# Turning the gated head outputs to channels by transposing DMAs instead of TensorE

## The chip, the core and the metric

One core of a Trainium2 chip runs the whole layer. The metric is the device time of one execution in microseconds. PE is TensorE, DVE is VectorE, ACT is ScalarE, POOL is GpSimd, SP is SyncE, which mainly issues transfers.

## The reference

One decoder layer on 512 tokens of 1,024 channels: a norm, a wide input projection, a convolution branch, a gated linear attention branch (GLA), a gated merge, and a feed-forward block. The change touches the end of the GLA branch:

```python
o = _gla_chunked(qh, kh, vh, gkh)                 # 512 tokens x 4 heads x 256
o = o * lax.rsqrt(jnp.mean(o * o, axis=-1, keepdims=True) + EPS) * gla_norm_g[l]
o = o.reshape(bsz, seq, GLA_VDIM) * jax.nn.silu(r)
y_gla = o @ w_gla_out[l]
merged = jax.nn.sigmoid(gate_a) * y_conv + jax.nn.sigmoid(gate_b) * y_gla
```

## The kernel before

All matrix products are in fp32 with both operands split into a high part (rounded to fp32r) and a low part (the rest), so that a product is three matmuls (`mm3`, L537: the weight's low part with the activation's high part, high with low, high with high). Weights are loaded by SP as 512 KB tiles (`raw`, four buffers), ACT casts them into `whi`, DVE subtracts to get `wlo` (`split_weight`, L414). `order` (L244) is the list of weights in the order of use, and SP's queue takes the loads in this order as buffers come free (`load`, `refill`).

The head outputs `ot[t, n]` are held with tokens on partitions: t is one of four tiles of 128 tokens, n one of two halves of 512 channels. The gate r is computed by `seven("w_r", ...)` (L1453), a product with seven instead of eight half sized steps (`a11, a12, s1, n2, s4, n3, a22`). `put_r` (L1544) takes each finished piece: ACT applies silu, and DVE multiplies the piece before it into `ot` (L1561, the last one at L1565). The pieces finish in the order (t,n) = (0,0), (1,0), (0,1), (1,1), (2,1), (3,1), (2,0), (3,0).

The output projection (`tile_of("w_gla", m, ...)`, L1444) needs the result with channels on partitions. `gated_o(m, bank)` (L1246) does this for channel tile m: four 128x128 transposes on PE into a PSUM bank, then ACT multiplies by the norm's gain into the high part `hi` and DVE forms the low part `lo`. Eight such tiles are needed, m = 0 to 3 from n = 0 and m = 4 to 7 from n = 1. Two are turned at the end of the r stage (`r_at`), the others two at a time inside the following pair of merge gate tiles.

That pair is `pair_7(0)` (L1579): the gate tiles w_gb 6 and 7 computed together by `two_tiles` (L1344) in four parts called x1, x3, x2, x4. They are accumulated in the three PSUM banks x, y, z, in steps of twelve matmuls with 256 columns. Bank x is read out between its steps (`put` and `combine`, L1350 to L1354) while later steps keep adding to it, so a step on x waits for the readout of the step before. Behind the pair come the projection tiles w_gla 0 and 1 (`PLAIN_GLA`, L1628), then the pair w_ga 0 and 1. POOL forms sums of weight tiles for such pairs (L398). Within the engines a scheduler sets the order when the kernel is built; on the chip each engine runs its instructions in that order.

Of the kernel before, what the change touches and what calls it, by code (L numbers as in the profile page):

```python
# [11 lines left out]
F32R = mybir.dt.float32r  # L12
BF16 = mybir.dt.bfloat16
U8 = mybir.dt.uint8
AF = mybir.ActivationFunctionType
ALU = mybir.AluOpType

P = 128
# [82 lines left out]
def trunk_layer(ctx: ExitStack, tc: tile.TileContext, a: dict, out: bass.AP):  # L101
    nc = tc.nc

    def pool(name, bufs, space=None):
        kw = {"space": space} if space is not None else {}
        return ctx.enter_context(tc.tile_pool(name=name, bufs=bufs, **kw))
# [20 lines left out]
    def nm(s):  # L127
        return f"{s}_{next(names)}"
# [137 lines left out]
    for gi, pairs in enumerate(GROUPS):  # L266
# [6 lines left out]
        tight |= set(range(first, len(order)))  # L273
        order += [("w_down", (pairs, step, d)) for step, d in STEPS]
    ready, raws = [], []
    pair_raws = {}
    kept = {}
    used = [0]
# [2 lines left out]
    def load():  # L281
        if len(raws) < len(order):
            name, j = order[len(raws)]
            if name in SEVEN:
                raws.append(load_block(name, *j))
                return
            if name == "two":
                name, p, q, part = j
                if part == "x1":
                    pair_raws[name, p] = [raw_tile() for _ in range(2)]  # L290
                    for raw, m in zip(pair_raws[name, p], (p, q)):
                        nc.sync.dma_start(raw, a[name][m])
                raws.append(None)
                return
            raw = raw_tile()
            nc.sync.dma_start(raw, a[name][j])
            raws.append(raw)

    def refill():

# [241 lines left out]
        nc.tensor.matmul(acc, lh, rl, start=False, stop=False, **kw)  # L542
        nc.tensor.matmul(acc, lh, rh, start=False, stop=last, **kw)  # L543

    def col_tile(w, acts, acc=None, lo=0, hi=T, at={}, ks=range(KT)):

        if acc is None:
            acc = mm_bank()
        for k in ks:
            s = slice(k * P, (k + 1) * P)  # L550
            ah, al = acts[k]
            mm3(acc[:, lo:hi], (w[0][:, s], w[1][:, s]), (ah[:, lo:hi], al[:, lo:hi]), k == 0, k == KT - 1)
            if k in at:
                at[k]()
        return acc
# [687 lines left out]

    ot = {}

    def gated_o(m, bank):  # L1246
        po = bank()
        c = (m % 4) * P
        for p in range(NT):
            nc.tensor.transpose(po[:, p * P : (p + 1) * P], ot[p, m // 4][:, c : c + P], ident)  # L1250
# [5 lines left out]
        hi, lo = (both[:, 0, :], both[:, 1, :]) if m < 4 else (heap(F32R), heap(F32R))  # L1256
        nc.scalar.activation(hi, po, AF.Copy, scale=gain)
        low_at[:] = [nc.vector.scalar_tensor_tensor(lo, po, gain, hi.bitcast(F32), ALU.mult, ALU.subtract)]
        oa[m] = hi, lo

    part = [None] * KT

# [178 lines left out]
    merged_tiles = {}  # L1441
    outs = {"w_gla": (lambda: oa, gla_out), "w_conv": (lambda: ca, conv_out)}

    def tile_of(name, m, ks, acc=None):  # L1444
        if acc is None:
            acc = (weight(name, m), mm_bank())
        col_tile(acc[0], outs[name][0](), acc[1], ks=ks)
        if KT - 1 in ks:
            outs[name][1](m, acc[1])
        return acc  # L1450

# [88 lines left out]
    def sums_for(step):  # L1540
        while urgent and step in ("s1", "n2", "s4", "n3") and step not in merge_acts:
            urgent.pop(0)[1]()

    def put_r(step, t, n, acc):  # L1544
        if step in ("a11", "s1", "n2"):
            rt[t, n] = rp_.tile([P, T], F32, tag="r", name=nm("r"), bufs=6)
            return nc.scalar.copy(rt[t, n], acc)
        if step == "a22":
            rt[t, n] = rp_.tile([P, T], F32, tag="r", name=nm("r"), bufs=6)
            nc.scalar.activation(rt[t, n], acc, AF.Silu)  # L1550
        else:
            r = rt[t, n]
            one, two = (r, acc) if step == "n3" else (acc, r)
            done = nc.vector.tensor_tensor(r, one, two, ALU.add if step == "a12" else ALU.subtract)
            nc.scalar.activation(r, r, AF.Silu)
        if step == "a22":
            done = None
        with tc.issue_after(done.ins) if done else ExitStack():
            while gated:
                i, j = gated.pop()  # L1560
                nc.vector.tensor_tensor(ot[i, j], ot[i, j], rt[i, j], ALU.mult)  # L1561
        gated.append((t, n))
        if (step, t, n) == ("a22", 3, 0):
            i, j = gated.pop()
            nc.vector.tensor_tensor(ot[i, j], ot[i, j], rt[i, j], ALU.mult)  # L1565
        return done if step == "n3" else None

    def r_at(step, i):
        if (step, i) == ("a22", 1):
            for m in range(4, 6):  # L1570
                gated_o(m, ax_bank)

    seven("w_r", R_PAIRS, [ByTile(k) for k in range(4)], None, r_at, put=put_r, before=sums_for)
    half_of = [range(KT // 2), range(KT // 2, KT)]
    open_tiles = {}

# [2 lines left out]
    def pair_7(n):  # L1579
        (name, p, q), behind = MERGE[n], BEHIND[n]  # L1580
        unit = two_tiles(name, p, q, lambda: merge_acts, mm_bank, len(behind) < 3)
        if behind and behind[0][0] == "w_conv":
            while chains:
                fill(1)
        for j in range(4):
            while urgent and j and len(urgent) > (5 if j == 1 else 0):
                urgent.pop(0)[1]()
            done = next(unit)
            if n == 0 and j == 2:
                while len(after) > 1:  # L1590
                    fill(1)
            if n == 0 and j < 3:
                for m in ((6, 7), (0, 1), (2, 3))[j]:
                    gated_o(m, ax_bank)
                if j == 2:
# [426 lines left out]
```

## Time and profile before

| | us |
|---|---|
| time, median of 3 runs (lowest to highest) | 817.37 (816.91 to 817.74) |
| the profiled execution | 816.96 |
| its span, from the first to the last instruction | 815.3 |
| PE busy in the span | 807.5 |
| transposes of the gated outputs, first and last start | 284.2 and 296.2 |
| first projection tile w_gla begins | 297.70 |

Times in the timeline count from the span's start. Each row names the start, the length, the engine, the line, the operation, and output<-input. A matmul's length overlaps with the next one, so the step from start to start is what counts on PE. `SPq`, `ACTq` and `POOLq` are the issuing of transfers by these engines.

### The profile page before, as it was taken

To read this page: it belongs to the slowest core of one execution; us is meant where nothing else is said; L and a number is where in the kernel's file an instruction comes from. 1 tells how busy PE (TensorE), PEld (TensorE's weight loads), DVE (VectorE), ACT (ScalarE), POOL (GpSimd) and SP (SyncE) were. 2 spreads that over 40 slices of the span, in tenths; PEclk is the share of its full clock that TensorE was granted. 3 is DMA by queue.
4 is the path that set the end of the run, shared out by engine and by line. 5 is a ranking of instruction groups with operands and counts; after the bars stand their busy time and mean duration, and the time that the engine had idled before them with its cause. 6 is when DMAs were issued, how large, how long until landed. Compare 5 with 4: busy or idle time off the path is not lost.

```text
span 815.3 us, 11441 instructions
## 1 busy us (share of the span) xinstructions
PE 807.5 (99%) x4215; PEld 693.2 (85%) x4215; DVE 700.7 (86%) x1108; ACT 487.9 (60%) x746; POOL 192.5 (24%) x166
## 2 busy tenths in 40 slices
PE   9999999999999999999999999999999999999996
PEld 7888888788888898989888898898889988899885
DVE  6679999998998988486779899979976999789896
ACT  6667788677546575494435655556435663466655
POOL 2025433332204332122001100320133300522010
PEclk9999999999999999999999999999999999999999
DMA  8487858745831232432458613145732345334662
GB/s 337 146 198 179 187 160 176 161 119 135 186 95 60 78 130 78 137 105 95 164 124 220 190 57 126 52 154 156 144 127 92 142 117 167 105 104 171 165 129 105
DMA packets 36616, 113.60 MB, mean 139 GB/s; under 512 B 3704, under 2 KB 8960, under 8 KB 36560
## 3 DMA queue, kind: packets, MB, share of 16 engines
q1 hardware_dynamic: 29200, 86.92, 30.8%
q0 software_dynamic: 7200, 25.69, 18.0%
q8 instruction: 33, 0.54, 0.3%
q14 instruction: 23, 0.19, 0.1%
q10 hardware_dynamic: 160, 0.27, 0.1%
HBM read 110.76 MB, written 2.10 MB: 138 GB/s over the span
## 4 chain that ended last, share of the span: by engine, by line
PE 84%; DVE 13%; issue 1%; ACT 1%; DMA 1%; SPq 0%; DVEq 0%; ACTq 0%
PE mm L541 20%; PE mm L542 20%; PE mm L543 20%; DVE c L902 5%; PE cv L541 4%; PE cv L542 4%; PE cv L543 4%; DVE aside L902 3%; PE ax L542 2%; PE ax L541 2%; PE ax L543 2%; PE ax L1230 1%; PE ax L1232 1%; DMA kept<-in_w_r_dram 1%; PE ax L1212 0%
## 5 line engine op out<-in xcount | busy, mean ns | idle before, releaser
L541 PE MATMUL mm<-uh,wlo 128*128 128x512 f32 (+1 forms) x532 | 193.9, 364 | 0.2 <-DVE wlo L464 0.2
L542 PE MATMUL mm<-ul,whi 128*128 128x512 f32 (+1 forms) x532 | 191.6, 360 | 0.0
L543 PE MATMUL mm<-uh,whi 128*128 128x512 f32 (+1 forms) x532 | 191.4, 360 | 0.0
L427 DVE TENSOR_TENSOR wlo<-raw,whi 128x1024 fp32r<-128x1024 f32 x82 | 96.0, 1178 | 36.0 <-ACT whi L426 32.2
L398 POOL TENSOR_TENSOR raw<-raw,raw 128x512 f32<-128x512 f32 x39 | 63.9, 1638 | 236.3 <-DVE wlo L427 130.9
L541 PEld LDWEIGHTS mm<-uh,wlo 128*128 128x128 f32 x532 | 100.5, 189 | 15.6 <-DVE wlo L464 0.6
L543 PEld LDWEIGHTS mm<-uh,whi 128*128 128x128 f32 x532 | 100.4, 189 | 15.4
L542 PEld LDWEIGHTS mm<-ul,whi 128*128 128x128 f32 x532 | 100.5, 189 | 14.7
L426 ACT CAST whi<-raw 128x1024 fp32r<-128x1024 f32 x82 | 78.9, 965 | 41.4 <-PE mm L543 24.4
L456 ACT CAST whi<-raw 128x1024 fp32r<-128x1024 f32 x80 | 83.5, 1048 | 27.5 <-PE mm L543 13.9
L464 DVE TENSOR_TENSOR wlo<-raw,whi 128x1024 fp32r<-128x1024 f32 x50 | 66.3, 1331 | 7.1 <-ACT whi L456 6.8
L426 ACT CAST whi<-kept 128x1024 fp32r<-128x1024 f32 (+1 forms) x40 | 40.1, 1008 | 32.4 <-DVE kept L374 16.5
L902 DVE SCALAR_TENSOR_TENSOR aside<-cv,pp,aside 128x255 f32<-128x255 f32 (+6 forms) x112 | 52.2, 466 | 0.0
L902 DVE SCALAR_TENSOR_TENSOR c<-aside,btmp,c 128x247 f32<-128x247 f32 (+13 forms) x93 | 52.1, 565 | 0.0
L427 DVE TENSOR_TENSOR wlo<-kept,whi 128x1024 fp32r<-128x1024 f32 (+1 forms) x40 | 47.5, 1191 | 4.9 <-ACT whi L426 4.7
L902 DVE SCALAR_TENSOR_TENSOR c<-cv,pp,c 128x247 f32<-128x247 f32 (+13 forms) x93 | 43.2, 465 | 1.4 <-ACT c L898 1.4
L458 ACT ACTIVATE wlo<-raw 128x1024 fp32r<-128x1024 f32 x28 | 29.4, 1059 | 19.1 <-PE mm L541 19.1
L1351 ACT COPY tmp<-mm 128x256 f32<-128x256 f32 x38 | 14.1, 370 | 35.1 <-PE mm L543 34.3
L1733 DVE SCALAR_TENSOR_TENSOR tmp<-mm,pp,tmp 128x511 f32<-128x511 f32 (+1 forms) x42 | 31.2, 743 | 3.5 <-ACT tmp L1730 3.4
L1733 DVE SCALAR_TENSOR_TENSOR tmp<-tmp,pp,tmp 128x511 f32<-128x511 f32 (+1 forms) x32 | 27.8, 888 | 0.3
L1504 DVE TENSOR_TENSOR hres<-hres,mm 128x512 f32<-128x512 f32 (+1 forms) x37 | 24.7, 676 | 2.2 <-PE mm L543 2.1
L542 PE MATMUL cv<-ul,whi 128*128 128x512 f32 (+1 forms) x72 | 25.6, 356 | 0.0
(514 smaller groups left out, 2078.3 us busy)
## 6 DMA issues: line engine op xcount, KB each, us to landing
raw<-in_w_up_dram SPq DMA_DIRECT2D x44, 512.0 KB, 3.2
raw<-in_w_glu_dram SPq DMA_DIRECT2D x16, 512.0 KB, 5.1
raw<-in_w_down_dram SPq DMA_DIRECT2D x16, 512.0 KB, 3.4
wlo<-in_w_glu_dram POOLq DMA_DIRECT2D x12, 512.0 KB, 7.1
kept<-in_w_down_dram POOLq DMA_DIRECT2D x9, 512.0 KB, 5.5
raw<-in_w_v_dram SPq DMA_DIRECT2D x8, 512.0 KB, 6.0
raw<-in_w_qk_dram SPq DMA_DIRECT2D x8, 512.0 KB, 6.3
raw<-in_w_gb_dram SPq DMA_DIRECT2D x8, 512.0 KB, 4.0
```

What stands on the lines that cost most here:

```text
L398: work = nc.gpsimd.tensor_tensor(out, x, y, ALU.add)
L426: nc.scalar.copy(hi, raw)
L427: two_low[:] = [nc.vector.tensor_tensor(lo, raw, hi.bitcast(F32), ALU.subtract)]
L456: nc.scalar.copy(hi, raw)
L458: pace[0] = nc.scalar.mul(lo, raw, -1.0)
L464: pace[0] = nc.vector.tensor_tensor(lo, raw, hi.bitcast(F32), ALU.subtract)
L541: nc.tensor.matmul(acc, ll, rh, start=first, stop=False, **kw)
L542: nc.tensor.matmul(acc, lh, rl, start=False, stop=False, **kw)
L543: nc.tensor.matmul(acc, lh, rh, start=False, stop=last, **kw)
L902: nc.vector.scalar_tensor_tensor(out[:, j:], x[:, : half_t - j], w, out[:, j:], ALU.mult, ALU.add)
L1504: done = nc.vector.tensor_tensor(hres[t, n][:, c], hres[t, n][:, c], acc[:, c], op)
L1733: nc.vector.scalar_tensor_tensor(z[:, s:], acc[:, : T - s], w[j], z[:, s:], ALU.mult, ALU.add)
```

## The change

Every gated piece `ot[t, n]` (fp32) is taken as 16 bit words. ACT copies it into two planes, the even and the odd words of each partition (`words`, 1,024 words per partition), and a DMA stores the planes as two rows per token into a buffer in device memory, `halves_of_words[n]`, 1,024 rows of 512 words. The stores go out from POOL for t = 0 and 1, from SP for t = 2 and 3 with n = 1, from ACT for t = 2 and 3 with n = 0. When all rows of a half are there, one transposing DMA per channel tile (`turn_o`, on SP) brings 128 columns of the 1,024 rows back, so that channels are on partitions and each token's two words lie side by side again, as fp32. `split_o` then forms the high and low part with the gain as before, with `turned[m]` in SBUF as source instead of a PSUM bank. The 32 transposes on PE are gone. Weight loads except w_gla 0 and 1 are put behind the last transposing DMA issued so far. The plain projection tiles take their k steps in the order 4 to 7, 0 to 3.

```diff
+    dram = pool("dram", 1, bass.MemoryType.DRAM)
...
+    def fetch(raw, name, j):
+        early = (name, j) in (("w_gla", 0), ("w_gla", 1))
+        with tc.issue_after(last_turn[0].ins) if last_turn and not early else ExitStack():
             nc.sync.dma_start(raw, a[name][j])
...
-    def gated_o(m, bank):
-        po = bank()
-        c = (m % 4) * P
-        for p in range(NT):
-            nc.tensor.transpose(po[:, p * P : (p + 1) * P], ot[p, m // 4][:, c : c + P], ident)
-        gain = pp[:, PP_GG + m % 2 : PP_GG + m % 2 + 1]
...
-        nc.scalar.activation(hi, po, AF.Copy, scale=gain)
-        low_at[:] = [nc.vector.scalar_tensor_tensor(lo, po, gain, hi.bitcast(F32), ALU.mult, ALU.subtract)]
+    halves_of_words = [dram.tile([2 * T, DV * 2], U16, name=nm("words")) for _ in range(2)]
+
+    def words(t, n):
+        if t > 1:
+            if t == 2:
+                tag, bufs = ("x", 3) if n else ("gain", 1)
+                late_planes[n] = tp.tile([P, 2, 2, T], U16, tag=tag, name=nm("planes"), bufs=bufs)
+            planes = late_planes[n][:, t - 2]
+        else:
+            planes = tp.tile([P, 2, T], U16, tag="btmp", name=nm("planes"), bufs=2)
+        after_gate[1:] = [nc.scalar.copy(planes, ot[t, n].bitcast(U16).rearrange("p (c two) -> p two c", two=2))]
+        rows = halves_of_words[n][2 * t * P : 2 * (t + 1) * P, :]
+        queue = nc.gpsimd if t < 2 else nc.sync if n else nc.scalar
+        queue.dma_start(rows.rearrange("(p two) c -> p two c", two=2), planes)
+
+    def turn_o(m):
...
+        c = (m % 4) * P
+        last_turn[:] = [nc.sync.dma_start(turned[m].bitcast(U16), halves_of_words[m // 4][:, c : c + P], transpose=True)]
+
+    def split_o(m):
+        hi, lo = oa[m]
+        gain = pp[:, PP_GG + m % 2 : PP_GG + m % 2 + 1]
...
+            nc.scalar.activation(hi, turned[m], AF.Copy, scale=gain)
+            low_at[:] = [nc.vector.scalar_tensor_tensor(lo, turned[m], gain, hi.bitcast(F32), ALU.mult, ALU.subtract)]
...
+    def gate_o(t, n):
+        after_gate[:] = [nc.vector.tensor_tensor(ot[t, n], ot[t, n], rt[t, n], ALU.mult)]
+        words(t, n)
...
             while gated:
-                i, j = gated.pop()
-                nc.vector.tensor_tensor(ot[i, j], ot[i, j], rt[i, j], ALU.mult)
+                gate_o(*gated.pop())
         gated.append((t, n))
         if (step, t, n) == ("a22", 3, 0):
+            for m in range(4, KT):
+                turn_o(m)
+            gate_o(*gated.pop())
+            for m in range(4):
+                turn_o(m)
...
-            if n == 0 and j < 3:
-                for m in ((6, 7), (0, 1), (2, 3))[j]:
-                    gated_o(m, ax_bank)
+            if n == 0:
+                for m in ((), (4, 5), (6, 7), (0, 1, 2, 3))[j]:
+                    split_o(m)
...
-            tile_of("w_gla", m, range(KT))
+            tile_of("w_gla", m, [*range(KT // 2, KT), *range(KT // 2)], ends=(KT // 2, KT // 2 - 1))
```

The first place is ACT's queue around the end of the r stage and the start of the pair w_gb 6 and 7. In both pieces `r` is a piece of the gate in silu, `raw_2644`, `raw_2687` and `raw_2645` are the weights of the pair's parts before, and the first `tmp<-mm` copy is the readout of bank x. Before:

```order
L1555 ACTIVATE r_2545<-r_2545 128x512
L426 CAST whi_2683<-raw_2644 128x1024
L426 CAST whi_2691<-raw_2687 128x1024
L1555 ACTIVATE r_2559<-r_2559 128x512
L1550 ACTIVATE r_2708<-cv_2412 128x512
L426 CAST whi_2750<-raw_2645 128x1024
L1550 ACTIVATE r_2741<-mm_2413 128x512
L1257 ACTIVATE h_2728<-ax_2723,pp 128x512
L426 CAST whi_2800<-raw_2687 128x512
L1257 ACTIVATE h_2737<-ax_2732,pp 128x512
L1351 COPY tmp_2748<-mm_2745 128x256
```

In the changed kernel the same stretch from the cast of the pair's second weight on, where `h_2131` to `h_1612` are the gated pieces (1,1), (2,1), (3,1), (2,0) and (3,0) and `planes` the 16 bit planes:

```order
L434 CAST whi_2710<-raw_2706 128x1024 [waits PE_49,Pool_49]
L1592 ACTIVATE r_2566<-r_2566 128x512 [waits DVE_49]
L1266 COPY planes_2681<-h_2131 128x1024 [waits DMASW6_49,Activation_49]
L1266 COPY planes_2699<-h_2133 128x1024 [waits DMAHW1_49,DVE_49]
L1587 ACTIVATE r_2727<-cv_2416 128x512 [waits PE_49]
L434 CAST whi_2785<-raw_2658 128x1024 [waits DMAHW6_49,PE_49,Pool_49]
L1266 COPY planes_2699<-h_2135 128x1024 [waits DVE_49]
L1587 ACTIVATE r_2744<-mm_2417 128x512 [waits PE_49]
L1266 COPY planes_2747<-h_1610 128x1024 [waits DVE_49]
L1266 COPY planes_2747<-h_1612 128x1024 [waits DVE_49]
L1269 DMA words_1285<-planes_2747 128x1024 [waits Activation_49] x2
L1384 COPY tmp_2783<-mm_2780 128x256 [waits PE_49]
```

Five plane copies and two DMA issues now stand ahead of the readout of bank x, and the copies with gain are behind it. The copy of (1,1) waits for a store issued by POOL (DMASW6).

The second place is POOL's queue there, in the changed kernel; before, the four sums stand in the same order without the DMAs:

```order
L406 TENSOR_TENSOR raw_2706<-raw_2657,raw_2658 128x512
L406 TENSOR_TENSOR raw_2706<-raw_2706,raw_2658 128x512
L406 TENSOR_TENSOR raw_2658<-raw_2658 128x512
L1269 DMA words_1285<-planes_2631 128x1024
L1269 DMA words_1286<-planes_2649 128x1024
L1269 DMA words_1286<-planes_2681 128x1024
L406 TENSOR_TENSOR raw_2706<-raw_2706,raw_2657 128x512
```

The stores of (1,0), (0,1) and (1,1) come behind three sums of the pair's weights and ahead of the fourth.

The third place is SP's queue from the load of the first projection weight on. Before:

```order
L296 DMA raw_2754<-in_w_gla_dram 128x1024
L296 DMA raw_2804<-in_w_gla_dram 128x1024
L292 DMA raw_2852<-in_w_ga_dram 128x1024
L292 DMA raw_2853<-in_w_ga_dram 128x1024
L296 DMA raw_2906<-in_w_gla_dram 128x1024
```

And in the changed kernel, where `words_1286` is the half n = 1 and `words_1285` the half n = 0:

```order
L305 DMA raw_2789<-in_w_gla_dram 128x1024 [waits DMAHW7_49,DMAHW0_49,DVE_49]
L1269 DMA words_1286<-planes_2699 128x1024 [waits Activation_49]
L305 DMA raw_2821<-in_w_gla_dram 128x1024 [waits DMAHW5_49,DMAHW1_49,Pool_49]
L1269 DMA words_1286<-planes_2699 128x1024 [waits DMAHW2_49,Activation_49]
L1283 DMA_TRANSPOSE turned_2752<-words_1286 128x1024 [waits DMAHW0_49,DMAHW2_49,DMASW7_49,DMASW6_49]
L1283 DMA_TRANSPOSE turned_2756<-words_1286 128x1024 [waits DMAHW6_49]
L1283 DMA_TRANSPOSE turned_2760<-words_1286 128x1024 [waits DMAHW7_49]
L1283 DMA_TRANSPOSE turned_2764<-words_1286 128x1024 [waits DVE_49]
L1283 DMA_TRANSPOSE turned_2770<-words_1285 128x1024 [waits DMAHW3_49,DMAHW1_49,DMAHW5_49,DMASW5_49,DMASW4_49]
...
L1283 DMA_TRANSPOSE turned_2778<-words_1285 128x1024 [waits DMAHW4_49,DVE_49]
L305 DMA raw_2857<-in_w_ga_dram 128x1024
L305 DMA raw_2858<-in_w_ga_dram 128x1024 [waits DMAHW6_49,DVE_49]
```

The last store of each half and the eight transposing DMAs, which wait for all stores of their half, stand between the second projection weight and the weights of the next gate pair.

More of the change, by code (lines that the diff above doesn't have):

```diff
@@ L543, in mm3, with col_tile @@
         nc.tensor.matmul(acc, lh, rh, start=False, stop=last, **kw)
-    def col_tile(w, acts, acc=None, lo=0, hi=T, at={}, ks=range(KT)):
+    def col_tile(w, acts, acc=None, lo=0, hi=T, at={}, ks=range(KT), ends=(0, KT - 1)):
         if acc is None:
@@ L1255, in gated_o @@
             both = tp.tile([P, 2, T], F32R, tag="gain", name=nm("oa"), bufs=1)
[L1256 to L1259, printed above, removed]
+        oa[m] = (both[:, 0, :], both[:, 1, :]) if m < 4 else (heap(F32R), heap(F32R))
+        if m == 0:
+            both = rp_.tile([P, 2, T], F32, tag="rx", name=nm("turned"), bufs=1)
+            turned[0], turned[1] = both[:, 0, :], both[:, 1, :]
+        elif m > 1:
+            turned[m] = rp_.tile([P, T], F32, tag="r", name=nm("turned"), bufs=6)
+        c = (m % 4) * P
[3 more added lines that the diff above has]
+        gain = pp[:, PP_GG + m % 2 : PP_GG + m % 2 + 1]
+        with ExitStack() as order_of:
+            for ins in after_gate:
+                order_of.enter_context(tc.issue_after(ins.ins))
+            nc.scalar.activation(hi, turned[m], AF.Copy, scale=gain)
+            low_at[:] = [nc.vector.scalar_tensor_tensor(lo, turned[m], gain, hi.bitcast(F32), ALU.mult, ALU.subtract)]
     part = [None] * KT
@@ L1559, in put_r @@
             while gated:
[L1560 to L1561 removed]
+                gate_o(*gated.pop())
         gated.append((t, n))
         if (step, t, n) == ("a22", 3, 0):
[L1564 to L1573 removed]
+            for m in range(4, KT):
[3 more added lines that the diff above has]
+                turn_o(m)
+        return done if step == "n3" else None
+    seven("w_r", R_PAIRS, [ByTile(k) for k in range(4)], None, put=put_r, before=sums_for)
     half_of = [range(KT // 2), range(KT // 2, KT)]
```

20 lines of the change are left out of this document (12 added, 8 removed).

## The prediction

> **What bounds the kernel now.** I read the busy times first, then the list of who waited for whom, the chain that ended last, and last the timelines of the engines around the place of the change.
>
> ```profile
> PE 807.5 (99%) x4215; PEld 693.2 (85%) x4215; DVE 700.7 (86%) x1108; ACT 487.9 (60%) x746; POOL 192.5 (24%) x166
> ...
> PE mm L661 <- DVE ones L634: 1.1, 1, 1.1
> PE mm L541 <- DVE wlo L464: 0.2, 1, 0.2
> ```
>
> TensorE (PE) is busy for 807.5 of 815.3 us, and its two waits in the list come to 1.3 us. So each microsecond taken from PE counts, and so does each microsecond for which PE must newly wait: nowhere later is there idle time that would give it back. The chain runs through PE, and these are its pieces that the change removes:
>
> ```profile
> 284.33 0.87 PE ax L1250 x8
> 288.08 0.87 PE ax L1250 x8
> 291.82 0.87 PE ax L1250 x8
> 295.56 0.87 PE ax L1250 x8
> ```
>
> **What goes.** Four groups of eight transposes, 4 x 0.87 = 3.48 us, all on the path. That is the whole possible gain. The eight copies with gain on ScalarE (ACT) and the eight subtractions on VectorE (DVE) stay, with another source; changing the order of the k steps in the projection costs nothing.
>
> **What the freed time falls on.** The second view is PE's timeline, the third busy time by stretch.
>
> ```profile
> 284.17 1.03 PE L1250 MATMUL ax<-ident,h 128*128 128x128 f32 x8
> ...
> 285.28 0.28 PE L543 MATMUL mm<-uh,whi 128*128 128x256 f32 x1
> 285.40 0.28 PE L541 MATMUL mm<-uh,wlo 128*128 128x256 f32 x1
> ...
> 297.70 0.40 PE L541 MATMUL mm<-oa,wlo 128*128 128x512 f32 x1
> ...
> 302.26 0.39 PE L543 MATMUL mm<-h,whi 128*128 128x512 f32 x1
> 302.49 0.39 PE L541 MATMUL mm<-h,wlo 128*128 128x512 f32 x1
> 270.00:284.10 14.10, 13.98 (x62) 11.29 (x61) 13.68 (x15) 7.97 (x10) 6.62 (x4) 1.00 0.13 46
> 284.10:297.70 13.60, 13.60 (x118) 13.53 (x116) 10.99 (x15) 10.44 (x18) 1.12 (x2) 1.00 0.48 156
> ```
>
> The pair of gate tiles is 84 matmuls (24, 24, 24 and 12), one every 0.12 us (285.28 to 285.40). It starts at 284.17 without the transposes and would end at 297.70 - 3.48 = 294.2, where the first projection tile needs the turned outputs. A step of that tile is three matmuls of 0.23 us (302.26 to 302.49), its eighth begins at 302.49 in this trace. ACT (columns: busy time after PE, PEld and DVE) is 7.97 of 14.10 us busy before the pair and 10.44 of 13.60 us in it. Into these 27.7 us the change puts seven of its eight copies into 16 bit planes.
>
> **Step 1: the copies on ACT.** A plane copy writes 1,024 elements per partition; no row has it. The nearest is the cast of 1,024 elements.
>
> ```profile
> 275.67 0.63 ACT L1555 ACTIVATE r<-r 128x512 f32<-128x512 f32 x1 [1.46 <-DVE r L1554]
> ...
> 279.05 1.99 ACT L426 CAST whi<-raw 128x1024 fp32r<-128x1024 f32 x2
> ...
> 286.68 0.37 ACT L1351 COPY tmp<-mm 128x256 f32<-128x256 f32 x1
> 275.57 1.18 DVE L1561 TENSOR_TENSOR h<-h,r 128x512 f32<-128x512 f32 x1
> ```
>
> I take 1.0 us a copy (1.99 for two) and 0.6 us for each silu; the other end for the copy is 0.6 us, the price of 512 elements. The four copies for the first two token tiles share a buffer: each of them waits in the order of ACT for the store of the one before, on the DMASW semaphores, and GpSimd (POOL) issues these stores. The store of (1,0) stands there behind the sums of the weight pair:
>
> ```profile
> 270.97 2.98 POOL L398 TENSOR_TENSOR raw<-raw,raw 128x512 f32<-128x512 f32 x2 [11.87 <-DMA raw<-in_w_gb_dram]
> 273.91 2.28 POOL L398 TENSOR_TENSOR raw<-raw 128x512 f32<-128x512 f32 x1
> L356 POOL DMA_DIRECT2D raw<-in_w_down_dram x6: 847/857/883, 571.5 to 783.2; - x6
> raw<-in_w_down_dram POOLq DMA_DIRECT2D x1, 256.0 KB, 3.8
> out_dram<-hres SPq DMA_DIRECT2D x2, 256.0 KB, 2.0
> out_dram<-y ACTq DMA_DIRECT2D x1, 256.0 KB, 2.7
> L1837 ACTq DMA_DIRECT2D out_dram<-y x1: 382/382/382, 811.6 to 811.6; - x1
> ```
>
> It is issued at 273.91 + 2.28 = 276.2. A 256 KB transfer of that queue lands in 3.8 us (it adds as it writes), a 256 KB store of SyncE in 2.0 us: I take 3.8 because it is the same queue, and keep 2.0. So the copy of (0,1), whose product is ready at 275.57 + 1.18 = 276.8, starts at 280.0 and not at 276.8, and all of ACT stands behind it. From there ACT has in its order: that copy, a silu, two weight casts and a silu (280.0 + 1.0 + 0.6 + 2.0 + 0.6 = 284.2); the copy of (1,1), which waits for the store issued at 281.0 and landed at 284.8; the copy of (2,1), to 286.8; a silu, a cast, a copy (289.4); a silu and two copies (292.0); two DMA issues of 0.38 (292.8); and then the copy of PE's bank x, 0.37, at 293.1.
>
> **Step 2: who waits for that.** The pair's second step adds onto bank x and may not start before that copy. PE reaches it after 36 matmuls, at 284.17 + 36 x 0.12 = 288.5 (the order already puts the step on bank y ahead of it). It waits 4.6 us. The 48 matmuls behind it take 5.8 us, so the projection starts at 298.9 instead of 294.2. Sum so far: -3.5 + 4.7 = **+1.2 us**. With stores of 2.0 us ACT is never empty after 278.2, its list is 12.5 us long and ends at 290.7: sum -1.3 us.
>
> **Step 3: the turns.** The last store of the second half (3,1) goes out on SyncE's queue when its copy is done, 289.4, behind the load of a projection weight; with 2.6 us, between the two stores' 2.0 and 2.7 and beside that load, the first turn starts at 292.0. The four of the first half need the stores issued by ACT, 292.8 + 2.7 = 295.5. Each turn moves 256 KB in 1,024 rows of 256 bytes. No row shows a transposing transfer. The smallest pieces in the trace are the 1 KB ones of a w_r load; these are the transfers of the window 252.0 to 256.5:
>
> ```profile
> DMA packets 528, 0.52 MB, mean 117 GB/s; under 512 B 16, under 2 KB 528, under 8 KB 528
> q1 hardware_dynamic: 528, 0.52, 35.6%
> raw<-in_w_r_dram SPq DMA_DIRECT2D x1, 512.0 KB, 3.3
> ```
>
> 0.356 x 16 x 4.5 us / 528 = 48.5 ns a piece. By bytes a 256 byte piece is 12.1 ns and a turn (64 pieces on each of 16 engines) 0.78 us; by pieces it is 48.5 ns and a turn 3.1 us. The ends are a factor of four apart and the row lies at one of them in size and at the other in rate, so I take the middle in ratio, 1.55 us, and keep both. After the last byte comes what a 2.0 us store has beyond its 0.78 us of moving, 1.2 us; then the high and the low part:
>
> ```profile
> L1257 ACT ACTIVATE oa<-ax,pp x4: 678/686/692, 293.1 to 297.1; 128x512 fp32r<-128x512 f32 x4
> L1258 DVE SCALAR_TENSOR_TENSOR oa<-ax,pp,oa x4: 743/745/751, 293.8 to 298.9; 128x512 fp32r<-128x512 f32 x4
> ```
>
> The eighth is ready at 292.0 + 8 x 1.55 + 1.2 + 1.4 = 307.0. PE, started at 298.9, wants it at 298.9 + 21 x 0.23 = 303.7, and had it at 302.49 before. So the eighth step comes 307.0 - 302.5 = **4.5 us** later than before, and this contains the 1.2 of step 2. Loads of the next gate pair stand behind the turns on SyncE's queue: issued by 304.4, landed about 3.7 us later, cast and split by 311; PE needs them after the second projection tile (24 x 0.23 = 5.5 us), at 313: covered, with 2 us to spare. On DVE the first low part stands ahead of the subtraction that reads bank x before the pair's last step; the first turn lands at 292.0 + 1.55 + 1.2 = 294.8, its low part is done at 296.2, the last step starts at 298.9 - 1.4 = 297.5: covered by 1.3 us. On POOL the store issued at 285.8 (0.86 us) puts the sum for the pair's last step back to about 289; ACT casts it at 293.1: covered. Behind the high parts on ACT stands the cast of the second projection weight, wanted a whole tile later.
>
> [...]
>
> **The sum.** The profiled execution took 816.96 us (815.3 of span, 1.7 around it); it would be 821.5. The median before is 817.37, so I forecast 817.37 + 4.5 = **821.9 us**. Chance 0.40.
>
> **The rivals.**
>
> Quick turns, price by bytes: the eighth is ready at 301.1 (from 295.5, four turns, 1.2 and 1.4), PE wants it at 303.7, only step 2 counts: +1.2, 818.6 us, or 816.1 with the quick stores. For it speaks that a 1 KB piece has no visible fixed cost; against it that a 256 byte piece has not been seen. Chance 0.22, half of it within the bound below.
>
> The clock falls in the wait of step 2. After PE's last work, at about 809.1, these rows give the granted clock (seventh column group, after the busy times):
>
> ```profile
> 809.00:812.00 3.00, 0.10 (x1) 0.00 (x0) 2.25 (x8) 0.88 (x3) 0.20 (x1) 0.92 0.43 175
> 812.00:815.30 3.30, 0.00 (x0) 0.00 (x0) 0.00 (x0) 0.00 (x0) 0.00 (x0) 0.50 0.42 161
> ...
> 4.77 1.63 PE L669 MATMUL ax<-ident,x 128*128 128x128 f32 x8
> ...
> 8.17 1.04 PE L669 MATMUL ax<-ident,x 128*128 128x128 f32 x8
> ```
>
> 0.92 means 2.5 of 3.0 us at full clock, then half: about 2.4 us idle is enough, and step 2 waits 4.6. At the start eight transposes take 1.63 us until 6.4 and 1.04 us from 8.2, so work from 1.1 to 6.4 was slow, 5.3 us, half of it lost: 2.6 us. [...] In my forecast the 2.6 us vanish in the wait for the turns (303.7 + 2.6 = 306.3, before 307.0). With quick turns they show: 818.6 + 2.6 = 821.2 us. Chance 0.08.
>
> Slow turns, each piece at the price of a 1 KB one: the eighth at 292.0 + 24.8 + 1.2 + 1.4 = 319.4, +16.9, 834.3 us. For it: the transposition may need one piece per row whatever its length. Chance 0.18.
>
> Faster: the plane copies cost 0.6 us and not 1.0, and the stores land in 2.0 us. Then ACT's list from 278.2 is six copies shorter by 0.4 each, 10.1 us, and bank x is free at 288.3, before PE asks for it; with quick turns nothing waits and the 3.48 us are gained: 813.9 us. It decides as soon as PE's wait is under 1.9 us. Against it: a cast of 1,024 elements takes 1.0 us, source and target in the same memory. Chance 0.12.
>
> **The numbers.** About 0.2%, 1.6 us, is what a measurement here can tell from no change. Faster: 0.12. Same: half of the quick turns, 0.11. Slower: 0.77. The range goes from the faster case to the slow turns, 813.9 to 834.3, and leaves out half of each, 0.15.
>
> **What would show it.** Right: in the changed trace PE idles some 4 us at the pair's second step with the copy of bank x named as what ended it, plane copies near 1.0 us, and a second wait inside the first projection tile ended by the high or low part of a turned tile, the turns landing about 1.5 us apart. Wrong: no idle PE between 284 and 300; turns under 1 us apart; or a wait at the next gate pair's weights, which I cost at nothing.

## The result, and the profile after

| | us |
|---|---|
| before, median of 4 runs beside the new ones (lowest to highest) | 817.39 (816.91 to 817.74) |
| after, median of 4 runs | 825.60 (824.03 to 826.24) |
| ratio, 95% interval | 1.0098 (1.0081 to 1.0115) |
| the profiled execution after, its span | 825.84, 823.9 |

Of the runs further below, two fell into a slower state, one of the kernel ilv_order (1,639.72 us) and one of the kernel before beside it (1,154.99 us); they are left out of the ratios and of ilv_order's median.

The kernel became 8.2 us slower. The forecast was 821.9 us with a range of 813.9 to 834.3: the sign is right, the size is 3.7 us short. The page of the changed kernel, busy times:

```profile
PE 808.5 (98%) x4183; PEld 691.8 (84%) x4183; DVE 704.5 (86%) x1108; ACT 498.1 (60%) x756; POOL 194.9 (24%) x170
```

PE has 32 instructions fewer, but 1.0 us more of busy time and 15.4 us of span in which it is not busy (7.8 before). The list of waits around the change (who waited, for what: us in total, times, longest) says where:

```profile
PE mm L549 <- ACT h L1291: 4.2, 1, 4.2
...
PE mm L549 <- ACT tmp L1384: 2.0, 1, 2.0
...
PE mm L549 <- DVE tmp L1387: 1.1, 1, 1.1
```

The timeline of PE puts them in order: the pair's first matmul, its second step on bank x, its last step, the first projection tile, that tile's fourth step (m = 7), its fifth (m = 0), its eighth (m = 3), and the next gate pair.

```profile
284.94 0.28 PE L549 MATMUL mm<-uh,wlo 128*128 128x256 f32 x1
...
291.41 0.38 PE L549 MATMUL mm<-hq,wlo 128*128 128x256 f32 x1 [2.00 <-ACT tmp L1384]
...
297.18 0.39 PE L549 MATMUL mm<-uh,wlo 128*128 128x256 f32 x1 [1.06 <-DVE tmp L1387]
...
298.71 0.40 PE L549 MATMUL mm<-h,wlo 128*128 128x512 f32 x1
...
305.45 1.22 PE L549 MATMUL mm<-h,wlo 128*128 128x512 f32 x2 [4.19 <-ACT h L1291]
...
307.75 0.63 PE L549 MATMUL mm<-oa,wlo 128*128 128x512 f32 x1
...
311.18 0.40 PE L549 MATMUL mm<-oa,wlo 128*128 128x512 f32 x1
...
316.88 0.28 PE L549 MATMUL mm<-uh,wlo 128*128 128x256 f32 x1
```

The first projection tile starts at 298.71, 1.0 us later than before (297.70). Its eighth step starts at 311.18, 8.7 us later than before (302.49). So the first two waits, the pair's start (0.8 us later than the 284.17 at which it could follow without the transposes) and some slower first matmuls behind each wait eat the 3.48 us of transposes and 1 us more, and nearly all of the loss arises inside the projection tile. ACT's timeline names the cause. Rows `h` are the high parts of m = 4 to 7, rows `oa` those of m = 0 to 3:

```profile
279.95 1.05 ACT L1266 COPY planes<-h 128x1024 uint16<-128x1024 uint16 x1 [3.95 <-DVE h L1578]
...
290.99 0.37 ACT L1384 COPY tmp<-mm 128x256 f32<-128x256 f32 x1 [0.41 <-ACT planes L1266]
...
298.50 0.73 ACT L1291 ACTIVATE h<-turned,pp 128x512 fp32r<-128x512 f32 x1 [0.42 <-DMA turned<-words]
302.73 0.72 ACT L1291 ACTIVATE oa<-turned,pp 128x512 fp32r<-128x512 f32 x1 [3.50 <-DMA turned<-words]
...
304.07 0.72 ACT L1291 ACTIVATE oa<-turned,pp 128x512 fp32r<-128x512 f32 x1 [0.35 <-DMA turned<-words]
304.69 0.71 ACT L1291 ACTIVATE h<-turned,pp 128x512 fp32r<-128x512 f32 x1
...
306.77 0.72 ACT L1291 ACTIVATE oa<-turned,pp 128x512 fp32r<-128x512 f32 x1 [0.34 <-DMA turned<-words]
```

After m = 6 (298.50) ACT has in its order m = 0, then m = 1, and only then m = 7. PE reads 4, 5, 6, 7, 0 and so on. ACT stands 3.50 us idle for the turn of m = 0, while m = 7, turned before it, stands behind it. And while PE waits, its clock falls (busy time of PE, PEld, DVE, ACT, POOL, then the granted clock, DMA share, GB/s):

```profile
291.40:298.70 7.30, 6.22 (x48) 5.95 (x49) 4.52 (x8) 5.07 (x9) 0.00 (x0) 1.00 0.89 178
303.00:304.00 1.00, 0.00 (x0) 0.00 (x0) 0.51 (x1) 0.71 (x2) 0.00 (x0) 0.92 0.95 174
304.00:310.00 6.00, 4.55 (x11) 3.58 (x12) 3.67 (x6) 5.25 (x7) 0.00 (x0) 0.50 0.98 299
310.00:311.00 1.00, 1.00 (x5) 0.79 (x4) 0.59 (x1) 0.91 (x2) 0.18 (x1) 0.67 0.30 123
```

From 305.45 to about 310.7 PE works at half clock, a matmul every 0.43 us instead of 0.23: 5.2 us, about half of them (2.6) lost. After the first wait, which was 2.00 us, the clock stayed at 1.00 in this execution (first row). The instructions by tile (minimum/median/maximum ns of one) price the copies and the turns:

```profile
L1266 ACT COPY planes<-h x8: 1027/1044/1046, 260.5 to 289.5; 128x1024 uint16<-128x1024 uint16 x8
L1283 SPq DMA_TRANSPOSE turned<-words x8: 1235/1298/3077, 291.5 to 302.9; - x8
```

And the transfers, KB of each and median us from issue to landing:

```profile
words<-planes POOLq DMA_DIRECT2D x3, 256.0 KB, 2.3
...
turned<-words SPq DMA_TRANSPOSE x8, 4.2
```

### The profile page after: what moved, and what is told of

It reads as the page before. It is cut to its first block, busy times and chain, and to the rows that moved or that the text cites. A ratio compares the mean times of both kernels' runs of the same rounds, so it can differ in the third digit from the quotient of the medians.

```text
span 823.9 us, 11421 instructions
## 1 busy us (share of the span) xinstructions
PE 808.5 (98%) x4183; PEld 691.8 (84%) x4183; DVE 704.5 (86%) x1108; ACT 498.1 (60%) x756; POOL 194.9 (24%) x170
## 3 DMA queue, kind: packets, MB, share of 16 engines
HBM read 110.76 MB, written 4.19 MB: 140 GB/s over the span
## 4 chain that ended last, share of the span: by engine, by line
PE 72%; DVE 15%; issue 5%; ACT 4%; DMA 1%; SPq 1%; POOL 1%; DVEq 0%; ACTq 0%; POOLq 0%
PE mm L549 17%; PE mm L550 17%; PE mm L551 17%; DVE c L910 5%; PE cv L550 4%; PE cv L551 4%; PE cv L549 4%; DVE aside L910 3%; PE ax L551 2%; PE ax L550 2%; PE ax L549 2%; DVE wlo L435 1%; PE mm L766 1%; ACT whi L434 1%; SPq L1283 1%
## 5 line engine op out<-in xcount | busy, mean ns | idle before, releaser
L435 DVE TENSOR_TENSOR wlo<-raw,whi 128x1024 fp32r<-128x1024 f32 x82 | 97.8, 1200 | 30.0 <-ACT whi L434 25.8
L406 POOL TENSOR_TENSOR raw<-raw,raw 128x512 f32<-128x512 f32 x39 | 61.3, 1572 | 230.6 <-DVE wlo L435 103.0
L551 PEld LDWEIGHTS mm<-uh,whi 128*128 128x128 f32 x532 | 100.4, 189 | 15.4
L472 DVE TENSOR_TENSOR wlo<-raw,whi 128x1024 fp32r<-128x1024 f32 x50 | 68.2, 1369 | 8.6 <-ACT whi L464 8.5
L406 POOL TENSOR_TENSOR raw<-raw 128x512 f32<-128x512 f32 x13 | 26.5, 2038 | 0.0
```

The source lines that it names most:

```text
L406: work = nc.gpsimd.tensor_tensor(out, x, y, ALU.add)
L435: two_low[:] = [nc.vector.tensor_tensor(lo, raw, hi.bitcast(F32), ALU.subtract)]
L472: pace[0] = nc.vector.tensor_tensor(lo, raw, hi.bitcast(F32), ALU.subtract)
```

## The experiments

All times are medians. Each ratio is to runs of the kernel before made beside that kernel: 817.25 us for none, copies, order and warm, 817.36 us for plain, halves, ilv_order and ilv_pool, and 817.60 us for the last three.

| kernel | us (lowest to highest) | ratio to before, 95% |
|---|---|---|
| none | 814.67 (814.34 to 815.44) | 0.9969 (0.9958 to 0.9980) |
| copies | 817.54 (816.89 to 818.20) | 1.0004 (0.9994 to 1.0013) |
| plain | 818.05 (815.20 to 818.73) | 1.0006 (0.9996 to 1.0016) |
| order | 822.62 (821.84 to 823.27) | 1.0064 (1.0047 to 1.0081) |
| warm | 822.93 (822.62 to 823.64) | 1.0070 (1.0055 to 1.0085) |
| halves | 828.81 (828.00 to 828.98) | 1.0137 (1.0121 to 1.0153) |
| ilv_order | 821.13 (820.72 to 821.67) | 1.0046 (1.0028 to 1.0064) |
| ilv_pool | 826.30 (825.68 to 826.88) | 1.0106 (1.0088 to 1.0124) |
| read_dve | 823.79 (823.48 to 824.33) | 1.0078 (1.0063 to 1.0093) |
| best | 821.28 (819.98 to 821.91) | 1.0044 (1.0029 to 1.0059) |
| two_queues | 835.45 (834.66 to 836.81) | 1.0216 (1.0199 to 1.0233) |

**none: what can be gained at all.** `split_o` reads the token tiles, and `words` and `turn_o` do nothing.

```diff
-        after_gate[1:] = [nc.scalar.copy(planes, ot[t, n]...)]
-        queue.dma_start(rows..., planes)
-        last_turn[:] = [nc.sync.dma_start(turned[m]..., transpose=True)]
+        turned[m] = ot[m % 4, m // 4]
```

> No plane copies, no stores and no transposing transfers: the high and low parts are formed from the token tiles as they are (left out: the turning to channels itself). Theory: PE's 3.48 us of transposes are all that the change can gain, so the time is 817.4 - 3.5 = 813.9 us, and PE has no wait from 284 to 312. Rival: the waits in the pair come from the weights or from the readouts in any case (the transposes only hid them): then PE still waits some 1 to 2 us at the pair's second step or at its last, and the time is 815 to 816 us.

814.67 us, 2.6 us under before, where 3.5 were expected. From the list of waits of PE, 200 to 330 us, the only row:

```profile
PE cv L549 <- DVE r L1583: 0.3, 1, 0.3
```

PE waits for nothing in the pair, so the rival falls too. A comparison of PE's timelines, start by start, shows that 3.1 of the 3.48 us are gained by the next gate pair, and that 0.3 us are lost again near 369 us; why these parts are lost is not shown. So about 2.6 us is what this change can win, with the other instructions in the order that the scheduler gives them here.

**copies: ACT's copies without any transfer.** As none, but with the plane copies kept.

> Only the plane copies on ACT are kept; no stores and no transposing transfers, the parts are formed from the token tiles (left out: the turning to channels itself). If the copies by themselves jam ACT, PE still waits at the pair's second step and starts the projection late: 0.8 us lost ahead of the pair and up to 3.7 us in it, 816 to 818 us. If the jam comes from the store that the third copy waits for (the 3.95 us of ACT ahead of it in the changed kernel), the copies alone cost under 1 us: 813.9 to 815 us.

817.54 us is 2.9 us over none, so the copies alone eat the whole gain. On ACT's timeline:

```profile
275.88 1.05 ACT L1266 COPY planes<-h 128x1024 uint16<-128x1024 uint16 x1 [0.53 <-DVE h L1577]
...
287.30 0.37 ACT L1383 COPY tmp<-mm 128x256 f32<-128x256 f32 x1
```

Without stores the copy of (0,1) follows its product at 275.88 and not at 279.95, and bank x is read out at 287.30, not at 290.99. So the 3.95 us for which ACT stood in the changed kernel were the wait for the store of (1,0): the DVE row that the trace names ended just then, but the product of (0,1) was long done. The copies' own price shows elsewhere: PE has two waits of 0.4 us for readouts on ACT and two of 0.5 and 0.7 us for low parts on DVE, and it is 0.3 us late ahead of the pair.

**plain: ordinary loads instead of turns.**

```diff
-        after_gate[1:] = [nc.scalar.copy(planes, ot[t, n].bitcast(U16).rearrange("p (c two) -> p two c", two=2))]
+        after_gate[1:] = [nc.scalar.copy(planes, ot[t, n].bitcast(U16).rearrange("p (two c) -> p two c", two=2))]
...
-        nc.sync.dma_start(turned[m].bitcast(U16), halves_of_words[m // 4][:, c : c + P], transpose=True)
+        plain = halves_of_words[m // 4][2 * c : 2 * (c + P), :].rearrange("(p two) c -> p two c", two=2)
+        nc.sync.dma_start(turned[m].bitcast(U16).rearrange("p (two c) -> p two c", two=2), plain)
```

> Plane copies, stores and waits stay, but each of the eight transposing transfers is an ordinary 256 KB load of the same buffer into the same tile (128 pieces of 2 KB; the copy keeps the words in their order; left out: the turning to channels). If the price of a transposing transfer is what makes the second wait, the loads land in about 2 to 3 us each and overlap, the eighth tile is there by 299, PE waits only for the readout of bank x (2.0 us and what follows it), and the time is 825.6 - 7.2 = 818.4 us. If the wait comes from the stores' landing and ACT's jam, the eighth step is still near 309 to 311 and the time 823 us or more.

818.05 us, as the first theory has it. PE waits for the readout of bank x, 2.0 us, and for nothing in the projection. The first row of its waits of PE, then its loads by tile and their landing:

```profile
PE mm L549 <- ACT tmp L1385: 2.0, 1, 2.0
PE cv L549 <- DVE r L1592: 0.3, 1, 0.3
```

```profile
L1284 SPq DMA_DIRECT2D turned<-words x6: 319/416/445, 287.2 to 295.0; - x6
...
DMA to landing us min/median/max: 2.8/3.1/4.7
```

At the median of these six, an ordinary load of 256 KB keeps SyncE for 0.42 us and lands in 3.1; a transposing one keeps it for 1.30 and lands in 4.2. The experiment has one flaw: a load of one tile here needs the words of one token tile, not of all four, so the first loads start earlier. The difference to the changed kernel, 7.6 us, is therefore an upper end for the transposing transfers.

**order: the high parts in PE's order.**

```diff
-            for ins in after_gate:
+            for ins in after_gate + last_high:
                 order_of.enter_context(tc.issue_after(ins.ins))
-            nc.scalar.activation(hi, turned[m], AF.Copy, scale=gain)
+            last_high[:] = [nc.scalar.activation(hi, turned[m], AF.Copy, scale=gain)]
```

> The eight high parts on ACT are kept in the order in which PE reads them, m = 4 to 7 and then 0 to 3. Theory: m = 7 had landed by about 300 and waited behind m = 0 and 1; now its high part starts near 300, PE waits only for the turns themselves, in pieces under 2 us that do not lower the clock; the eighth step comes near 307.3 instead of 311.18 and the time is 825.6 - 3.9 = 821.7 us. Rival: the turns are late as a whole, the wait moves to m = 0, stays over 2.4 us and still halves the clock: 824 to 825.6 us.

822.62 us, 3.0 us under the changed kernel, no run of the one overlapping with the other. On PE's timeline the fourth step waits 0.92 us and the eighth starts at 307.19:

```profile
302.00 0.49 PE L549 MATMUL mm<-h,wlo 128*128 128x512 f32 x1 [0.92 <-ACT h L1292]
...
307.19 0.40 PE L549 MATMUL mm<-oa,wlo 128*128 128x512 f32 x1
```

The theory holds in the main. But m = 7's high part starts at 301.23 and not near 300: on ACT's timeline of this execution it waits for its own turn, so what remains of PE's wait here is the price of that turn.

```profile
301.23 0.72 ACT L1292 ACTIVATE h<-turned,pp 128x512 fp32r<-128x512 f32 x1 [2.25 <-DMA turned<-words]
```

The theory also had waits under 2 us leave the clock as it is. The busy times by stretch show otherwise:

```profile
291.50:295.00 3.50, 3.50 (x19) 3.50 (x18) 1.92 (x2) 1.84 (x5) 0.00 (x0) 0.51 0.80 160
```

In this execution the clock fell after the first wait (0.51 over 3.5 us), though that wait was 1.96 us, no longer than in the changed kernel.

**warm: the clock alone.**

```diff
+    def spin():
+        bank = ax_bank()
+        for _ in range(18):
+            turn = nc.tensor.matmul(bank, ready[used[0] - 1][0][:, :P], acts1[0][0], start=True, stop=True)
+            tc.keep_in_program_order(turn)
...
+            at = {6: spin} if (n, m) == (0, 0) else {}
-            tile_of("w_gla", m, ...)
+            tile_of("w_gla", m, ..., at=at)
```

> Eighteen matmuls into an unused bank (4.1 us of PE, nothing reads them) stand between the third and the fourth step of the first projection tile, where PE waited 4.2 us. If the lowered clock costs time, the granted clock stays at 1.00 from 304 to 312, the 0.43 us per matmul go back to 0.23, and the time is 825.6 - 2.6 = 823.0 us. If the slow matmuls only fill time in which the later turns were awaited anyhow, the time stays within 0.5 us of 825.6.

822.93 us, 2.7 us less than the changed kernel. The wait is filled, its end is where it was, and the eighth step comes at 308.45 instead of 311.18:

```profile
301.39 4.25 PE L1663 MATMUL ax<-uh,whi 128*128 128x512 f32 x18
305.49 0.39 PE L549 MATMUL mm<-h,wlo 128*128 128x512 f32 x1
...
308.45 0.39 PE L549 MATMUL mm<-oa,wlo 128*128 128x512 f32 x1
```

By stretch, the clock is at 1.00 there; it fell after the first wait in this execution too:

```profile
292.50:296.50 4.00, 4.00 (x23) 4.00 (x22) 1.75 (x3) 2.14 (x4) 0.00 (x0) 0.57 0.75 150
304.00:312.00 8.00, 8.00 (x36) 6.35 (x35) 4.63 (x6) 6.74 (x9) 2.04 (x1) 1.00 0.72 230
```

**halves: a price by instruction or by rows.**

```diff
-        nc.sync.dma_start(turned[m].bitcast(U16), halves_of_words[m // 4][:, c : c + P], transpose=True)
+        for r in (slice(0, T), slice(T, 2 * T)):
+            nc.sync.dma_start(turned[m].bitcast(U16)[:, r], halves_of_words[m // 4][r, c : c + P], transpose=True)
```

> Sixteen transposing transfers of 512 rows in place of eight of 1,024 rows; same bytes and pieces. If SyncE's issue of about 1.3 us and the landing go by rows, each takes half (0.65 us) and the time is 825.6 us within 1. If they are a price of each instruction, sixteen take 21 us instead of 12.7, the eighth tile comes 8 us later and the time is 832 to 834 us.

828.81 us lies between the two, but for SyncE's issue the rows decide for the instruction. They are given by tile, and then on SyncE's timeline:

```profile
L1284 SPq DMA_TRANSPOSE turned<-words x16: 1122/1252/1899, 279.9 to 306.3; - x16
...
DMA to landing us min/median/max: 2.6/2.8/4.8
```

```profile
289.91 17.67 SPq L1284 DMA_TRANSPOSE turned<-words  x13
```

Half the rows take 1.25 us of SyncE, whole ones 1.30; thirteen in a row take 17.67 us, 1.36 each. The landing does go down with the rows, from 4.2 us at the median to 2.8. The time stays under 832 us since three of the sixteen were issued before all pieces were there and the thirteen began at 289.91, 1.6 us before the eight of the changed kernel.

**ilv_order: the rate of use set to the rate of the turns.**

```diff
-            tile_of("w_gla", m, [*range(KT // 2, KT), *range(KT // 2)], ends=(KT // 2, KT // 2 - 1))
+        both = {}
+        for k in [*range(KT // 2, KT), *range(KT // 2)]:
+            for m in PLAIN_GLA[0]:
+                both[m] = tile_of("w_gla", m, [k], both.get(m), ends=(KT // 2, KT // 2 - 1))
```

(for the first pair alone, with the edit of order)

> The two projection tiles w_gla 0 and 1 are interleaved by k step, and the high parts on ACT are kept in PE's order. PE then uses a turned tile for 1.38 us instead of 0.69, about as fast as the turns are issued (1.3 to 1.6 us). If the turns' rate is what PE waits for, the waits after 298.7 vanish, the eighth tile is wanted at 298.7 + 7 x 1.38 = 308.4 and there at about 307: 825.6 - 7.2 = 818.4 us, up to 1.7 us more where the clock falls in the first wait. If the order on ACT was all of it, the time is that of the kernel with the order alone, 822.6 us.

821.13 us is 1.5 us under order, where 4.2 were expected. The waits for turns are gone, as foreseen. PE's waits from 283 to 320 us are now:

```profile
PE mm L549 <- ACT tmp L1385: 2.0, 1, 2.0
PE mm L549 <- DVE tmp L1388: 1.0, 1, 1.0
PE mm L549 <- DVE h L1467: 0.6, 1, 0.6
PE mm L549 <- DVE wlo L435: 0.4, 1, 0.4
```

By PE's timelines, start by start, this kernel is 3.9 us behind none at the end of the two tiles, close to the 3.7 us that were expected (818.4 to 814.7), and 5.9 us behind by 330 us. So the shortfall arises in the next gate pair, of which the last two rows are a half: a weight whose load stands behind the turns on SyncE, and a product on DVE (L1467). Once PE is no longer late for them, these two become waits.

**ilv_pool: the copies on POOL.** As ilv_order, with `nc.gpsimd.tensor_copy` for `nc.scalar.copy` in `words`.

> As the kernel with interleaved projection tiles and ordered high parts, and the plane copies run on POOL instead of ACT. If ACT's list is what delays the readout of bank x, the 2.0 us of that wait, the 1.1 us of the one after it and the 0.8 us ahead of the pair go too: 818.4 - 3.9 = 814.5 us, the time without any turning. Rival: a POOL copy of 1,024 words takes 3 us or more (its sums of 512 elements take 1.7), the stores of the last pieces leave later and the turns with them, PE waits for the turns: 817 to 822 us.

826.30 us is worse than both ends. These are rows of ACT's timeline:

```profile
291.77 0.62 ACT L434 CAST whi<-raw 128x512 fp32r<-128x512 f32 x1 [5.30 <-POOL raw L406]
...
294.13 0.37 ACT L1385 COPY tmp<-mm 128x256 f32<-128x256 f32 x1 [1.74 <-POOL planes L1267]
```

POOL's weight sum for the pair's last step now stands behind four of the copies, and two of these waited for their buffers' stores. ACT stands 5.30 us for that sum, then for the last copies, since a store issue precedes the readout in its order. Bank x is read out at 294.13, after PE had waited 5.8 us. A copy takes POOL 1.0 to 2.1 us. The jam was moved, not removed.

**read_dve and best: the readout of bank x on DVE.** read_dve is the changed kernel with this edit, best is ilv_order with it and with the loads of w_ga 0 and 1 left ahead of the turns.

```diff
-        put(c1[:, t1], x)
+        put(c1[:, t1], x, nc.vector.tensor_copy if at_once and name == "w_gb" else nc.scalar.copy)
```

> The first readout of bank x in the pair w_gb 6 and 7 runs on DVE, behind the last product (done at about 289.5), instead of on ACT behind the plane copies. PE's wait at the second step falls from 2.0 us to about 0.6, and with it the fall of the clock that the 2.0 us brought in some executions; on ACT only m = 0 still stands ahead of m = 7. If the turns set the end of the first projection tile (the eighth tile ready at about 307.5 whatever PE did before), the first wait is hidden behind them and the time is that of the kernel with ordered high parts, 822.6 us, or 0.4 us less. If the waits add up, it is 822.6 - 1.4 = 821.2 us, and 819.5 us where the clock counts too.

> Ordered high parts, interleaved projection tiles, the readout of bank x on DVE, and the loads of w_ga 0 and 1 no longer held behind the turns. Against the kernel with the first two alone (821.4 us): 1.4 us of the first wait and 0.4 + 0.6 us of the waits behind the projection go, 819.0 us. What remains above the 814.7 us without any turning is the copies on ACT (2.9 us) and some ramps. If copies and turns could all be hidden, 815 us; if the loads ahead of the turns push them back, 820 us or more.

read_dve takes 823.79 us and best 821.28 us, no less than ilv_order (821.13). The edit missed its aim. On DVE the readout stands behind the last product, which waits for ACT; and though it runs at 288.63 instead of 290.99, the scheduler has also moved PE's step on bank x ahead of the one on bank y, which now begins at 290.64. So PE asks for the readout after 24 matmuls and not after 36, and waits about as long as before. These are rows of the timelines of DVE and PE in read_dve, and the waits of best:

```profile
288.63 0.41 DVE L1384 COPY tmp<-mm 128x256 f32<-128x256 f32 x1
```

```profile
289.10 0.39 PE L549 MATMUL mm<-hq,wlo 128*128 128x256 f32 x1 [1.82 <-DVE tmp L1384]
...
290.64 0.28 PE L549 MATMUL cv<-c,wlo 128*128 128x256 f32 x1
...
303.39 0.79 PE L549 MATMUL mm<-h,wlo 128*128 128x512 f32 x1 [3.02 <-ACT h L1291]
```

```profile
PE mm L549 <- DVE tmp L1385: 1.9, 1, 1.9
PE mm L549 <- ACT h L1292: 0.5, 1, 0.5
```

So neither run tells whether the first wait adds to the second. In best only one of the two loads went out ahead of the turns (at 289.45); SyncE issued the other behind them (at 305.25). read_dve does repeat the main finding: with one high part ahead of m = 7 on ACT instead of two, PE waits 3.02 us, and the clock falls for 7 us again.

**two_queues: turns from two engines.** `nc.scalar` issues the turns of m = 0 to 3.

> The turns of m = 0 to 3 are issued by ACT, those of m = 4 to 7 by SyncE as before. If the 1.3 us per turn is the issuing engine's own price, both run at 1.3 us side by side with a landing of about 4 us, and all eight are issued by about 299 instead of 304. If all turns share one limit behind the queues, an issue or a landing takes about twice as long while both run. The time says less, since ACT is blocked for 5 us by its issues: 823 to 828 us.

The time is 835.45 us, and there is no answer: SyncE had issued its four turns by 298.2, ACT stood on a semaphore of the same line (L1283) for 3.16 us, and its first turn starts at 301.50, so the two never issued side by side. A readout behind the turns in ACT's order makes PE wait 12.2 us.

```profile
L1283 SPq DMA_TRANSPOSE turned<-words x4: 1301/1386/2910, 291.1 to 296.9; - x4
L1283 ACTq DMA_TRANSPOSE turned<-words x4: 1255/1332/1879, 301.5 to 306.0; - x4
```

Whether the limit of 1.3 us lies in the queue or behind it stays open.

## Why the prediction was right or wrong

**Right: the price of the parts.**

| | foreseen | measured |
|---|---|---|
| a plane copy | 1.0 us | 1.04 us |
| copy of (0,1) starts | 280.0 | 279.95 |
| first turn is issued | 292.0 | 291.48 |
| SyncE's time for one turn | 1.55 us | 1.30 us at the median, 1.59 on average (12.7 us in all, one of the eight took 3.08) |
| projection tile starts | 298.9 | 298.71 |
| eighth tile has its high part | 306.3 (307.0 less 0.7 for the low part) | 307.5 |
| eighth tile has its low part | 307.0 | 308.3 |

The start of the copy of (0,1) was met by luck, by two errors that cancel: the store that it waits for was issued at 277.5 and not at 276.2, and landed in 2.3 and not in 3.8 us. That it is the store's wait was shown by copies. The eighth tile is 1.2 us late because a turn took longer to land than the sum has it: the last high part starts on the landing, at 306.77, which is 2.6 us after SyncE was done with the eight turns (291.48 + 12.7 = 304.2), where the sum has 1.2 us.

**Mis-sized, without effect on the sum: step 2.** The wait at bank x was 2.0 us and not 4.6, since the readout came at 290.99 and not at 293.1 (the store for the copy of (1,1) landed 1.1 us earlier than priced, and ACT's copies followed each other every 0.95 us, with the first of the two store issues beside them), and since PE began the pair 0.8 us later. That later start was not foreseen. The low part ahead of the subtraction on DVE, costed as covered by 1.3 us, was done at 296.8 (296.2 foreseen), but PE, less delayed by the first wait, was at the last step at 296.1 and not at 297.5, and waited 1.06 us for the subtraction behind it.

**Wrong: "the eighth is ready at 307.0", taken as the time at which PE runs the eighth step.** Step 3 followed when turned tiles are ready and assumed that ACT forms the high parts in the order in which PE reads them. The scheduler had put m = 0 and 1 ahead of m = 7, so PE stood at its fourth step until 305.45, with four more behind it. ACT's order, which is fixed when the kernel is built, shows this without any run; I had read it up to the readout of bank x and no further. In order, where the assumption was made true, the eighth step starts at 307.19 and the time is 822.6 us: the sum of 821.9 us is within 0.7 us of the time of that kernel. In part this is luck, since the late landing hardly shows there: a step begins on the high part alone, while the low part, with which the sum had it begin, is done at 307.57 in order.

**Wrong: the clock's 2.6 us that "vanish in the wait for the turns".** The size was right (2.6 us; 2.7 by warm), the place was not. The rival had the fall in the first wait, where later waits would hide it. In the profiled execution it came in the second, with nothing behind to hide it. The condition, "about 2.4 us idle is enough", was not right either: waits of about 2.0 us lowered the clock in the profiled executions of order, warm, plain, best and two_queues, and not in those of the changed kernel and ilv_order. What decides between them is not shown.

The slow stretches last about 3.4 us in order (3.50 us at 0.51) and in warm (4.00 us at 0.57), and about 6.8 us in the changed kernel (1.00 us at 0.92, 6.00 at 0.50, 1.00 at 0.67), each taken as a mix of full and half clock. After the 2.0 us wait such a stretch begins 0.5 us behind its end in order and 1.4 us in warm, so that the end of the wait alone does not set the start.

So of the 3.7 us missed, order's 3.0 and warm's 2.7 overlap: the wrong order made the wait of 4.2 us in which the clock fell, and either remedy brings the time to within 1.1 us of the forecast.

**The rivals.** Quick turns (0.78 us) and slow turns (3.1 us) are both out by the rows above. On average a turn brought its 256 KB in 1.59 us, 165 GB/s, but halves shows why no rate serves for the issue: 128 KB held SyncE for 1.25 us at the median, 256 KB for 1.30. "Faster" is out: even without the transfers the copies left nothing (copies). Loads of the next gate pair: covered here, as said, but only because PE was late (ilv_order).

## What to carry to other kernels

When an operand set is produced by one in-order engine and consumed by another, compare the two orders before adding up ready times: late items ahead of a ready one cost 3.0 us here, with the lowered clock that followed, of the 3.7 us that the sum was short. To see what a change can win at most, run the version that leaves all its new work out, and then add the parts one by one: here the ceiling was 2.6 us, and the copies alone cost 2.9. A wait of PE can cost more than its own length by the clock: the wait of 4.2 us cost 2.7 us more (warm), and a slow stretch of 3.4 us behind a wait of 2.0 us, as in order, loses an estimated 1.7 us, half its length, where no later wait hides it. Whether several short waits of the same sum cost less was not tested.

## What the runs showed of the hardware

- A transposing transfer held SyncE for about 1.3 us whether it turned 1,024 or 512 rows (1,298 ns in the changed kernel and 1,252 ns in halves, at the median). It landed in 4.2 us with 1,024 rows and in 2.8 us with 512. The longest of eight whole turns held it for 2.1 to 3.1 us (3,077 ns in the changed kernel, 3,066 in order, 2,130 in ilv_order, 2,899 in read_dve, 2,996 in best). An ordinary load of 256 KB, as much as a whole turn, held it for 0.42 us and landed in 3.1 us, at the median (plain).
- A wait of PE of 1.9 to 2.0 us lowered the clock in some profiled executions (order, warm, plain, best, two_queues) and not in others (the changed kernel, ilv_order). In each profiled execution with a wait of 3.0 us or more between 200 and 340 us it fell to 0.50 (3.02 us in read_dve, 3.19 and 3.92 in halves, 4.19 in the changed kernel, 5.85 in ilv_pool, 12.23 in two_queues). Slow stretches lasted about 3.4 us (order, warm, plain, best) or about 6.8 us (the changed kernel, read_dve, ilv_pool); halves had one of each. In two_queues, around the wait of 12.23 us, the clock stood at 0.50 for the whole of 299 to 312 us.
